# Recurrent layer's in-projections as float16 pairs, with block scales found on the chip

## The chip, the cores and the metric

The kernel runs on one core of one Trainium2 chip. The metric is the device time of one execution in microseconds; the kernel before took 1345.06 us (median of 3 runs, 1344.2 to 1348.67). Five engines work side by side, each through its own instructions in order: TensorE (PE, with its weight loads PEld), VectorE (DVE), ScalarE (ACT), GpSimd (POOL) and SyncE (SP), which issues the transfers.

## The reference, cut to what matters

Two layers process a prompt of 512 tokens and a sample of 32. Layer 0 mixes tokens by a recurrence (RWKV-7), layer 1 by differential attention. Each layer has one input projection, memory attention, a gate and an output projection.

```python
def rwkv_layer(x, mk, mv, prev_row, S0, norm_w, w_out, w_in, ...):
    h = rmsnorm(x, norm_w)
    p, qm, gate = jnp.split(h @ w_in, [RW_PROJ, RW_PROJ + MEM_W], axis=-1)
    y_mix, S_T, last_row = rwkv_mixer(p, prev_row, S0, ...)
    y_mem = mem_attention(qm, mk, mv)
    out = jnp.concatenate([y_mix, y_mem], axis=-1) * jax.nn.silu(gate)
    return x + out @ w_out, S_T, last_row
    ...
    def step(S, inp):
        r_t, k_t, v_t, w_t, kk_t, a_t = inp
        sa = jnp.einsum('bhvk,bhk->bhv', S, -kk_t)
        S = (S * w_t[:, :, None, :] + sa[..., None] * (kk_t * a_t)[:, :, None, :]
             + v_t[..., None] * k_t[:, :, None, :])
        return S, jnp.einsum('bhvk,bhk->bhv', S, r_t)
```

The change concerns `h @ w_in` of layer 0: 1024 rows by 7296 columns, for 544 tokens.

## The kernel before

All matrices stand with features on the 128 partitions and the 544 tokens along the free axis. The input projection of layer 0 is cut into 57 blocks of 128 output columns: 37 shifted rows (receptance, key, value for 12 head pairs, and one block for the low-rank parts), 4 queries, 16 gates. A block needs 1024 x 128 weights, 512 KB, in two half loads.

To keep float32 accuracy, an operand is split into a high and a low part, and a block is three products, high x high, high x low and low x high, over 8 slices of 128 rows and 2 halves of 272 tokens: 48 matmuls (`steps`, `gemm`). In layer 0 the parts are float32r, TensorE's faster float32 format: `hh`, `hl` for the normed tokens, `whi`, `wlo` for the weights. `split` makes the latter: ScalarE casts a half block, VectorE (the line `low.tensor_tensor`) subtracts. Layer 1 already uses float16 pairs. Since float16 has a narrow range, each weight block is scaled there by a power of two: `square_total` squares a half block on ScalarE with a running sum, `total_spread` adds the sums over the partitions by two one-column matmuls with a matrix of ones, `scales` takes the power of two on VectorE (three tiny instructions), `scaled` multiplies the raw block on GpSimd, `split_scaled` casts and subtracts, and the evacuation from PSUM multiplies by the inverse. `load_pair`, `measured`, `scaled_pool` belong to the same path; in the kernel before, `scaled_pool` is called between the layers.

Layer 0 runs in two parts. At the start (`inputs`, `lora_in`, three `shift` calls) the tokens are turned and normed, the memory keys are projected, and four in-projection blocks follow (36, 12, 0, 24). `weights` and `used` keep one split block and one loaded block ahead. There the order on each engine is left to the scheduler of the language. The remaining 53 in-projection blocks, the four memory value blocks and two output blocks form the generator `stream`: it loads two blocks ahead, and puts the casts and subtractions of the next block into a list of put-off work (`put_off`, `some`, `until`). From here on `self.ordered` holds, and each engine's order is that in which the program writes its calls.

What sets that order is the loop over 12 head pairs. Each pair runs a chain of 8 chunks in 23 links (`chunk`): TensorE multiplies, VectorE adds or ScalarE copies the result (`avz`, `sv`, `SB` are these operands), TensorE multiplies again. `PLAN` says which other work goes beside which link. Between links the loop issues matmuls of `stream`, spread by a reckoned time per matmul, `MAIN`, and per link, `HOP`; after each half link, `some` takes one or two put-off operations.

```python
while left and t + MAIN / 2 < (due[k + 1] if half else (due[k] + due[k + 1]) / 2):
    next(main)
    t += MAIN
    left -= 1
```

Of the kernel before, what the change touches and what calls it, by code (L numbers as in the profile page):

```python
# [43 lines left out]
STAT1, SPREAD1, POWER1, SCALE1 = (14, 27), 12, 32, (37, 41)  # L44
SPLITS2, SCALE2 = (7, 11, 13, 17), (33, 36)
# [32 lines left out]
HOP, MAIN = 0.27, 0.126  # L78
# [64 lines left out]
class Trunk:  # L143
# [190 lines left out]
    def square_total(self, rec, q):  # L334

        if q == 0:
            rec["st"] = self.sts[rec["n"] % 4]
            if rec["n"] < 3:
# [43 lines left out]
    def measured(self, rec):  # L382

        if "s" not in rec:
            for q in range(2):
                self.square_total(rec, q)
            ps = self.psx.tile([P, 512], F32, tag="x", name="ps_st")
            self.total_spread(rec, ps[:, 0:1], True)
            self.scales(rec)
            for q in range(2):  # L390
                self.scaled(rec, q)

    def split_scaled(self, rec):
# [4 lines left out]
        ks = [slice(q * KT // 2, (q + 1) * KT // 2) for q in range(2)]  # L398
        todo = [(lambda k=k: self.ae.copy(hi[:, k], raw[:, k]), 0.0) for k in ks]
# [77 lines left out]
    def proj(self, src, c0, evac):  # L477
        self.gemm([self.weights(src, c0)], [(self.hh, self.hl)], evac)
# [25 lines left out]
    def inputs(self):  # L504

        nc, a = self.nc, self.a
        with ExitStack() as ctx:
# [16 lines left out]
            self.ahead = [(a["w_mem_k"][0], 3 * P)] + [(a["rw_in"][0], j * P) for j in (36, 12, 0, 24)]  # L524
# [10 lines left out]
            self.consts_norm(parB)  # L535
            ss = p.tile([P, 7], F32, name="ss")
# [60 lines left out]
            for k in range(KT):  # L597
                h = p.tile([P, TP], F32, tag="hn", name="hn", bufs=3)
                self.ve.scalar_tensor_tensor(h[:], xT[k], self.nw[0][:, k : k + 1], pr[0][:], ALU.mult, ALU.mult)
                self.ae.copy(self.hh[:, k, :TP], h[:])  # L600
                (self.ve if k in (2, 5, 7) else nc.gpsimd).tensor_tensor(self.hl[:, k, :TP], h[:], self.hh[:, k, :TP].bitcast(F32), ALU.subtract)  # L601
                if k in (3, 6):
                    next(kv)
                if k == 1:
                    sh = [P, KT, TS]
                    hs = p.tile(sh, F32, name="hs")
                    self.ve.tensor_tensor(hs[:], xs[:], self.nw[0].unsqueeze(2).to_broadcast(sh), ALU.mult)
                    self.ve.tensor_tensor(hs[:], hs[:], pr[1][:, :TS].unsqueeze(1).to_broadcast(sh), ALU.mult)
                    self.ae.copy(self.hh[:, :, TP:], hs[:])
                    self.ve.tensor_tensor(self.hl[:, :, TP:], hs[:], self.hh[:, :, TP:].bitcast(F32), ALU.subtract)  # L610
# [8 lines left out]
    def shifted(self, j, tag, bufs, w=None):  # L619
# [4 lines left out]
        made = {}  # L624

        def evac(ps, v):
            self.ae.copy(raw[:, v.start + 1 : v.stop + 1], ps)
            if w is not None and v.start:
# [18 lines left out]
        if w is None:  # L647
            self.proj(self.a["rw_in"][0], j * P, evac)
# [426 lines left out]
    def gate(self, src, c0, g):  # L1075

        sg, _, evac = self.gate_evac(self.o1[g])
        self.proj(src, c0, evac)
        return sg

# [8 lines left out]
    def rw_finish(self, st):  # L1089
# [31 lines left out]
        self.ve.scalar_tensor_tensor(sg[:], sg[:], 0.5, bv[:], ALU.mult, ALU.mult)  # L1121
# [63 lines left out]
    def mem_block(self, i, kind, h, mh, ml, w, out, ps_pool, ps_tag):  # L1185
# [4 lines left out]
        ps = self.psg.tile([P, 512], F32, tag="g", name="ps_g")  # L1190
        for k in range(KT):
            for u, x in ((0, mh), (0, ml), (1, mh)):
# [7 lines left out]
                yield  # L1200

# [13 lines left out]

    def mem_head(self, i, h, w, cq, cg, p):

        st = {}
        it = self.mem_steps(st, i, h, p)
        for _ in range(3):  # L1220
            next(it)
        st["q"], evac = self.query_evac(p)
        self.proj(w, cq + h * P, evac)
        for _ in range(9):
            next(it)
        sg = self.gate(w, cg + h * P, 12 + h)
        st["gate"] = lambda: sg
        for _ in it:
            pass
# [267 lines left out]
    def layer0(self, mem):  # L1497
# [6 lines left out]
        with ExitStack() as ctx:  # L1504
# [40 lines left out]
            def add(pr, src, c0, make):  # L1545
                blocks.append((src, c0, make))
# [3 lines left out]
            def add_gate(pr, st, c0, n):  # L1550
                def make(wt):
                    sg, st["gate"], evac = self.gate_evac(self.sg[n % SGB])
                    yield from self.steps(wt, evac)
                add(pr, w, c0, make)

            def add_shift(pr, of, q):
# [3 lines left out]
                add(pr, w, (12 * q + of) * P, make)  # L1560

            def add_query(pr, h):
                def make(wt):
                    mems[h]["q"], evac = self.query_evac(self.ma if h % 2 else self.rb2)
                    yield from self.steps(wt, evac)
                add(pr, w, RW_PROJ + h * P, make)
# [40 lines left out]
            blocks += [b + (None,) for b in after[:2]]  # L1607

            def stream():
                raws = [self.load(*b[:2]) for b in blocks[:2]]  # L1610
                wt = self.split(raws.pop(0))
                for _ in wt[1]:
                    self.put_off(*_)
                for i, (_, _, make) in enumerate(blocks):
# [128 lines left out]
        with ExitStack() as ctx:  # L1743
# [45 lines left out]
            self.scaled_pool()  # L1789
# [24 lines left out]
    def scaled_pool(self):  # L1814

        nc, p = self.nc, self.h0
        self.hh, self.hl = (lambda t: (t[:, 0], t[:, 1]))(p.tile([P, 2, KT, T], F16, tag="hl", name="h16"))
# [15 lines left out]
        with nc.allow_low_precision("a bound, rounded before a power of two is taken from it"):  # L1833
            self.ae.activation(sq, self.nw[1], AF.Square, accum_out=st)
# [4 lines left out]
        self.ve.tensor_scalar(self.nwx, self.nw[1], sx, None, ALU.mult)  # L1839
# [664 lines left out]
    def run(self):  # L2504
# [15 lines left out]
        self.hh = hp.tile([P, KT, T], F32R, tag="hh", name="hh")  # L2520
        self.hl = hp.tile([P, KT, T], F32R, tag="hl", name="hl")
# [57 lines left out]
```

## Time and profile before

| | |
|---|---|
| median of 3 runs | 1345.06 us |
| profiled execution | 1347.07 us, its span 1345.4 us |
| mean granted TensorE clock | 0.991 of full speed |
| start and memory keys | 0 to about 45 us |
| recurrent layer | to about 700 us |
| output projection of layer 0 | about 700 to 800 us |
| layer 1 | about 800 to 1345 us |

Columns of the grouped rows are: line of the code (140 is a helper that all queues go through), engine, operation, output and inputs by tile name, shape and type, count; then busy us and mean ns of one; then the idle time of the engine just ahead of them and what ended it. In a timeline row come start, length (both us), engine, operation and how many alike follow each other. A matmul's length is a model that overlaps its neighbours, so distances between starts are the safer measure. The type `f32` on a matmul stands for both float32 and float32r; a plain float32 matmul leaves two records.

### The profile page before, as it was taken

To read this page: it belongs to the slowest core of one execution; us is meant where nothing else is said; L and a number is where in the kernel's file an instruction comes from. 1 tells how busy PE (TensorE), PEld (TensorE's weight loads), DVE (VectorE), ACT (ScalarE), POOL (GpSimd) and SP (SyncE) were. 2 spreads that over 40 slices of the span, in tenths; PEclk is the share of its full clock that TensorE was granted. 3 is DMA by queue.
4 is the path that set the end of the run, shared out by engine and by line. 5 is a ranking of instruction groups with operands and counts; after the bars stand their busy time and mean duration, and the time that the engine had idled before them with its cause. 6 is when DMAs were issued, how large, how long until landed. Compare 5 with 4: busy or idle time off the path is not lost. (4 is left out here: it accounts for less than half of the span.)

```text
span 1345.4 us, 32382 instructions
## 1 busy us (share of the span) xinstructions
PE 1298.5 (97%) x11786; PEld 1173.1 (87%) x11786; DVE 950.1 (71%) x2490; ACT 886.1 (66%) x2411; POOL 678.8 (50%) x1141
## 2 busy tenths in 40 slices
PE   6999999999999999999999999999999999999997
PEld 6998989999999999888899999888887887888885
DVE  6767667887787787767575355666698667987756
ACT  6665677777767867765554337777676776886652
POOL 1317765577557655860021007756555655654652
PEclk9999899999999999999999999999999999999999
DMA  7643223322322232233357445787777768774741
GB/s 235 188 114 82 62 71 88 79 70 78 88 64 69 77 99 64 63 96 98 108 158 215 131 130 152 166 186 156 165 175 169 171 159 183 171 169 111 223 150 67
DMA packets 417723, 171.56 MB, mean 128 GB/s; under 512 B 195145, under 2 KB 402514, under 8 KB 417562
## 3 DMA queue, kind: packets, MB, share of 16 engines
q1 hardware_dynamic: 417418, 168.96, 48.7%
q8 instruction: 93, 1.52, 0.5%
q14 instruction: 68, 0.56, 0.1%
q10 hardware_dynamic: 144, 0.52, 0.1%
HBM read 130.84 MB, written 41.92 MB: 128 GB/s over the span
## 5 line engine op out<-in xcount | busy, mean ns | idle before, releaser
L140 PEld LDWEIGHTS <-whs 128*128 128x128 f16 x3456 | 327.3, 98 | 67.4 <-issue 4.6
L140 PE MATMUL ps_g<-h,whs 128*128 128x272 f16 x2688 | 332.4, 279 | 1.0 <-POOL whs L140 1.0
L140 PE MATMUL ps_g<-hh,wlo 128*128 128x272 f32 x912 | 277.0, 304 | 1.5 <-DVE wlo L140 1.5
L140 PE MATMUL ps_g<-hh,whi 128*128 128x272 f32 x912 | 275.7, 303 | 0.9 <-ACT hh L140 0.9
L140 PE MATMUL ps_g<-hl,whi 128*128 128x272 f32 x912 | 271.7, 298 | 0.5 <-POOL hl L601 0.5
L890 POOL TENSOR_TENSOR tm<-u,m 102x84 f32<-102x84 f32 (+23 forms) x372 | 156.0, 419 | 166.2 <-DMA m<-sc 138.2
L140 PEld LDWEIGHTS ps_g<-hh,whi 128*128 128x128 f32 x912 | 174.8, 192 | 4.4 <-ACT hh L140 1.3
L140 PEld LDWEIGHTS ps_g<-hh,wlo 128*128 128x128 f32 x912 | 174.0, 191 | 4.9 <-DVE wlo L140 2.3
L140 PEld LDWEIGHTS ps_g<-hl,whi 128*128 128x128 f32 x912 | 174.1, 191 | 2.4 <-POOL hl L601 0.7
L892 POOL TENSOR_TENSOR u<-u,tm 102x84 f32<-102x84 f32 (+23 forms) x372 | 160.6, 432 | 29.1
L140 POOL TENSOR_TENSOR whs<-h16s,whs 128x512 f16<-128x512 f32 x126 | 147.6, 1189 | 48.3 <-ACT whs L140 46.6
L140 DVE TENSOR_TENSOR wlo<-raw,whi 128x512 fp32r<-128x512 f32 x178 | 128.4, 732 | 48.2 <-ACT whi L140 47.3
L140 ACT CAST whi<-raw 128x512 fp32r<-128x512 f32 x178 | 107.0, 616 | 35.4 <-issue 19.3
L140 POOL TENSOR_SCALAR h16s<-h16s 128x512 f32<-128x512 f32 x112 | 81.6, 741 | 93.7 <-DVE h16s L140 93.7
L140 ACT CAST whs<-h16s 128x512 f16<-128x512 f32 x144 | 84.8, 618 | 34.7 <-POOL h16s L140 33.1
L140 PE MATMUL ps_g<-hl,whs 128*128 128x272 f16 x768 | 94.1, 279 | 0.9 <-POOL whs L140 0.8
L140 ACT ACTIVATE junkw<-h16s 128x512 bf16<-128x512 f32 x138 | 86.5, 627 | 5.5 <-DMA h16s<-in_df_in_dram 4.9
L140 DVE SCALAR_TENSOR_TENSOR SB<-ps_c,dl,sd 64x64 f32<-64x64 f32 x168 | 47.4, 282 | 40.9 <-PE ps_c L140 37.4
L140 PE MATMUL ps_g<-lo,whi 128*128 128x272 f32 x256 | 73.9, 289 | 0.7 <-DVE lo L140 0.7
L140 PE MATMUL ps_g<-hi,whi 128*128 128x272 f32 x256 | 73.8, 288 | 0.7 <-ACT whi L140 0.7
L140 PE MATMUL ps_g<-hi,wlo 128*128 128x272 f32 x256 | 73.6, 288 | 0.2 <-DVE wlo L140 0.2
L140 ACT COPY sv<-ps_c 64x64 f32<-64x64 f32 x192 | 39.2, 204 | 39.8 <-PE ps_c L140 37.9
(420 smaller groups left out, 2943.6 us busy)
## 6 DMA issues: line engine op xcount, KB each, us to landing
raw<-in_rw_in_dram SPq DMA_DIRECT2D x114, 256.0 KB
h16s<-in_df_in_dram SPq DMA_DIRECT2D x112, 256.0 KB
raw<-in_w_out_dram SPq DMA_DIRECT2D x32, 256.0 KB
h16s<-in_w_out_dram SPq DMA_DIRECT2D x32, 256.0 KB
ptr<-pk SPq DMA_DIRECT2D x44, 160.0 KB
aT<-ptr SPq DMA_DIRECT2D x11, 640.0 KB
scr<-sg SPq DMA_DIRECT2D x96, 68.0 KB
out_dram<-scr SPq DMA_DIRECT2D x6, 1024.0 KB
```

What stands on the lines that cost most here:

```text
L140: return lambda *a, **k: self.trunk.tie(self, issue(*a, **k))
L890: nc.gpsimd.tensor_tensor(tm[:, :n, :wd], u3[:, :n, kx : kx + 1].to_broadcast(sh), m3[:, kx : kx + 1, kx + 1 :].to_broadcast(sh), ALU.mult)
L892: nc.gpsimd.tensor_tensor(u3[:, :n, kx + 1 :], u3[:, :n, kx + 1 :], tm[:, :n, :wd], ALU.add)
```

## The change

The 57 in-projection blocks of layer 0 go over to the float16 pairs of layer 1, with these differences (`self.plain`):

- `scaled_pool` is now called in `inputs` as well, for layer 0; the tokens `hh`, `hl` are float16 from the start.
- The raw block isn't multiplied by its scale on GpSimd. The scale goes into the cast (`activation` with a scale) and into the subtraction, which becomes a `scalar_tensor_tensor` on VectorE.
- Every block gets two squares on ScalarE, two one-column matmuls and three tiny VectorE instructions. In the stream the squares of block i + 3 are put off during block i, the one-column matmuls of block i + 2 go behind the 12th matmul of block i, its scale behind the 30th (`POWER0`).
- Loads of such blocks run up to four ahead instead of two, in four raw buffers in place of five half buffers. The squares' discarded output goes into another raw buffer for the first eight blocks, then into one fixed tile.
- Every evacuation multiplies by the inverse scale on ScalarE; the gate's factor one half takes it in.
- `MAIN` goes from 0.126 to 0.117.
- `gate` and `mem_head`, which nothing calls, are removed.

```diff
-HOP, MAIN = 0.27, 0.126
+HOP, MAIN = 0.27, 0.117
...
+            if self.plain:
+                if rec["n"] == 8:
+                    self.junk = self.wp.tile([P, KT, P], BF16, tag="wlo", name="junkw", bufs=2)[:]
+                rec["junk"] = self.raws[(rec["n"] + 1 + rec["n"] // 4) % 4].bitcast(BF16)[:, :, :P] if rec["n"] < 8 else self.junk
+            elif rec["n"] < 3:
...
+        if self.plain:
+            s, todo = rec["s"], []
+            for k in ks:
+                todo.append((lambda k=k: self.ae.activation(hi[:, k], raw[:, k], AF.Copy, scale=s), 0.0))
+                todo.append((lambda k=k: self.ve.scalar_tensor_tensor(lo[:, k], raw[:, k], s, hi[:, k], ALU.mult, ALU.subtract), LATER))
+            return (hi, lo, rec["inv"]), todo
...
         def evac(ps, v):
-            self.ae.copy(raw[:, v.start + 1 : v.stop + 1], ps)
+            self.ae.activation(raw[:, v.start + 1 : v.stop + 1], ps, AF.Copy, scale=w[2])
...
             def stream():
-                raws = [self.load(*b[:2]) for b in blocks[:2]]
-                wt = self.split(raws.pop(0))
...
+                bring(range(4))
+                squares = [lambda q=q: self.square_total(recs[2], q) for q in range(2)]
+                for fn in squares:
+                    self.put_off(fn)
+                wt, behind = self.split(recs[0]), None
...
                     self.until(todo[-1][0])
-                    if i + 2 < len(blocks):
-                        raws.append(self.load(*blocks[i + 2][:2]))
-                    nxt = self.split(raws.pop(0)) if raws else None
+                    for fn in squares[1:]:
+                        self.until(fn)
+                    if behind:
+                        self.scales(behind)
+                    bring(j for j in range(i + 2, i + 5) if j < i + 3 or j < len(blocks) and blocks[j][2] is not None)
+                    nxt = self.split(recs[i + 1]) if i + 1 < len(blocks) else None
...
+                    squares = [lambda q=q, rec=paired(i + 3): self.square_total(rec, q) for q in range(2)] if paired(i + 3) else []
+                    for fn in squares:
+                        self.put_off(fn)
+                    self.rec = behind = paired(i + 2)
...
-                        yield from make(wt)
+                        for n, _ in enumerate(make(wt)):
+                            yield
+                            if n == POWER0 and behind:
+                                self.scales(behind)
+                                behind = None
```

Three places show how instructions stand in a row before and now. The first is on ScalarE in the middle of layer 0, between two links of the chain of one head pair: `yt`, `sd` and `sv` are the chain's copies, `sg` the evacuation of a gate block, `whi` or `whs` the cast of a half block, `junkw` a square. Before:

```order
L140 COPY sv<-ps_c 64x64 x2
L140 COPY yt_104<-ps_c 64x128
L140 ACTIVATE sd<-SB_654,dl 128x128
L140 ACTIVATE sg_83<-ps_g 128x272
L140 CAST whi<-raw 128x512
L140 COPY sv<-ps_c 64x64 x2
```

Now, at the same link:

```order
L141 COPY sv<-ps_c 64x64 x2
L141 COPY yt_102<-ps_c 64x128
L141 ACTIVATE sd<-SB_682,dl 128x128
L141 ACTIVATE junkw,h16s<-h16s 128x512
L141 ACTIVATE sg_81<-ps_g,h16s 128x272
L141 ACTIVATE junkw,h16s<-h16s 128x512
L141 ACTIVATE whs<-h16s 128x512
L141 COPY sv<-ps_c 64x64 x2
```

Two squares have come between `sd` and the next `sv`.

The second is on VectorE in the same part: the subtractions `whs` of a block and the three instructions that make a later block's scale (`h16s`), ahead of the state update `SB`.

```order
L141 SCALAR_TENSOR_TENSOR whs<-h16s,whs 128x512
L141 TENSOR_TENSOR zr_87<-nk,de 128x4x128
L141 TENSOR_TENSOR zr_87<-nk,de 128x32
L141 TENSOR_SCALAR h16s<-ps_g 128x1
L141 TENSOR_SCALAR h16s<-h16s 128x1 x2
L141 SCALAR_TENSOR_TENSOR SB_679<-ps_c,dl,sd 64x64 x2
```

The three rows with `128x1` are new; they stand at once, not in the list of put-off work.

The third is on TensorE at the start, where the first in-projection block begins behind the memory key blocks (`mmh`, `mml`). Before:

```order
L140 MATMUL ps_g<-mmh,wlo 128x256
L140 MATMUL ps_mkt<-ident,memx 128x128 x2
L140 MATMUL ps_par<-ident,pA 128x121
L140 MATMUL ps_par<-ident,pC 128x38
L140 MATMUL ps_g<-hh,whi 128x272
L140 MATMUL ps_g<-hl,whi 128x272
```

Now:

```order
L141 MATMUL ps_g<-mmh,whi 128x256
L141 MATMUL ps_g<-mml,whi 128x256
L141 MATMUL ps_g<-mmh,wlo 128x256
L141 LDWEIGHTS h16s
L141 MATMUL ps_st<-h16s 128x1
L141 LDWEIGHTS whs
L141 MATMUL ps_g<-h_175,whs 128x272
```

A one-column matmul `ps_st` stands ahead of the first projection matmul. It is the fifth of eight at the start, the first half of the third in-projection block.

More of the change, by code (lines that the diff above doesn't have):

```diff
@@ L386, in measured @@
                 self.square_total(rec, q)
-            ps = self.psx.tile([P, 512], F32, tag="x", name="ps_st")
+            pool, tag = (self.psg, "g") if self.plain else (self.psx, "x")
+            ps = pool.tile([P, 512], F32, tag=tag, name="ps_st")
             self.total_spread(rec, ps[:, 0:1], True)
             self.scales(rec)
-            for q in range(2):
+            for q in () if self.plain else range(2):
                 self.scaled(rec, q)
@@ L523, in inputs @@
             self.early = [self.load(a["w_mem_k"][0], 2 * P)]
-            self.ahead = [(a["w_mem_k"][0], 3 * P)] + [(a["rw_in"][0], j * P) for j in (36, 12, 0, 24)]
+            self.ahead = [(a["w_mem_k"][0], 3 * P)] + [(a["rw_in"][0], j * P, 0) for j in (36, 12, 0, 24)]
             parA = self.params(
@@ L624, in shifted @@
         made = {}
+        ramp = w is None
+        if ramp:
+            w = self.weights(None, 0)
         def evac(ps, v):
-            self.ae.copy(raw[:, v.start + 1 : v.stop + 1], ps)
-            if w is not None and v.start:
+            self.ae.activation(raw[:, v.start + 1 : v.stop + 1], ps, AF.Copy, scale=w[2])
+            if not ramp and v.start:
                 self.put_off(tail)
@@ L1200, in mem_block @@
                 yield
+                n += 1
+                if n == SPREAD1 and self.rec is not None:
+                    self.total_spread(self.rec, ps[:, 480:481], False)
     def softmax(self, ps, n, p, tag, bufs):
@@ L1543, in layer0, with add @@
             blocks, each = [], [0] * NPAIR
-            def add(pr, src, c0, make):
-                blocks.append((src, c0, make))
+            def add(pr, src, c0, make, kind=None):
+                blocks.append((src, c0, kind, make))
                 if pr is not None:
@@ L1606, in layer0, with bring, paired @@
             after = self.w_out_blocks(0)
[L1607 removed]
+            blocks += [b + (None, None) for b in after[:2]]
             def stream():
[L1610 to L1611 removed]
+                recs = [None] * len(blocks)
+                def bring(js):
+                    for j in js:
+                        if j < len(blocks) and recs[j] is None:
+                            recs[j] = self.load(*blocks[j][:3])
+                def paired(j):
+                    return recs[j] if j < len(blocks) and blocks[j][2] is not None else None
+                bring(range(4))
[3 more added lines that the diff above has]
+                wt, behind = self.split(recs[0]), None
                 for _ in wt[1]:
                     self.put_off(*_)
[L1614 removed]
+                for i, (_, _, _, make) in enumerate(blocks):
                     wt, todo = wt
                     self.until(todo[-1][0])
[L1617 to L1619 removed]
+                    for fn in squares[1:]:
[4 more added lines that the diff above has]
+                    nxt = self.split(recs[i + 1]) if i + 1 < len(blocks) else None
                     for _ in nxt[1] if nxt else ():
                         self.put_off(*_)
+                    squares = [lambda q=q, rec=paired(i + 3): self.square_total(rec, q) for q in range(2)] if paired(i + 3) else []
+                    for fn in squares:
+                        self.put_off(fn)
+                    self.rec = behind = paired(i + 2)
                     if make is None:
```

61 lines of the change are left out of this document (23 added, 38 removed).

## The prediction

> **What bounds the kernel now.** I read the page first, for the engine that is never free.
>
> ```profile
> PE 1298.5 (97%) x11786; PEld 1173.1 (87%) x11786; DVE 950.1 (71%) x2490; ACT 886.1 (66%) x2411; POOL 678.8 (50%) x1141
> L140 PE MATMUL ps_g<-h,whs 128*128 128x272 f16 x2688 | 332.4, 279 | 1.0 <-POOL whs L140 1.0
> L140 PE MATMUL ps_g<-hh,wlo 128*128 128x272 f32 x912 | 277.0, 304 | 1.5 <-DVE wlo L140 1.5
> L140 PE MATMUL ps_g<-hh,whi 128*128 128x272 f32 x912 | 275.7, 303 | 0.9 <-ACT hh L140 0.9
> L140 PE MATMUL ps_g<-hl,whi 128*128 128x272 f32 x912 | 271.7, 298 | 0.5 <-POOL hl L601 0.5
> ```
>
> TensorE is busy for 97% of the span. The three rows with `hh` and `hl` are the products that the change turns to float16: 57 blocks of 48, that is 3 x 912 = 2736. The first `ps_g` row is layer 1, which already works on float16 pairs. The mean lengths overlap one another, so they say little; what a matmul costs is the distance between starts. Next, then, the busy time by stretches (us, busy PE, PEld, DVE, ACT, POOL with counts, clock, DMA share, GB/s).
>
> ```profile
> 33.00:50.00 17.00, 15.54 (x114) 14.20 (x113) 15.17 (x35) 9.57 (x24) 11.06 (x36) 1.00 0.65 191
> 200.00:550.00 350.00, 346.51 (x3524) 327.81 (x3524) 274.63 (x688) 256.50 (x737) 220.93 (x483) 0.99 0.30 78
> ```
>
> In the long middle of layer 0 TensorE lacks 3.5 of 350 us, VectorE works 78% and ScalarE 73%. So time saved per matmul shows in the total, as long as the other two keep up. The stretch from 33 to 50 us is the start, in which the first projection meets VectorE at 89%.
>
> **The pitch of a projection matmul.** From the timeline of TensorE, a run of 25 matmuls of layer 0 without anything between (first and last), and one of layer 1.
>
> ```profile
> 129.52 0.29 PE L140 MATMUL ps_g<-hl,whi 128*128 128x272 f32 x1
> ...
> 132.54 0.29 PE L140 MATMUL ps_g<-hl,whi 128*128 128x272 f32 x1
> 1264.24 0.19 PE L140 MATMUL ps_g<-h16s 128*128 128x1 bf16 x2
> 1264.30 2.94 PE L140 MATMUL ps_g<-hl,whs 128*128 128x272 f16 x24
> 1267.07 0.19 PE L140 MATMUL ps_g<-h16s 128*128 128x1 bf16 x2
> ```
>
> Layer 0: 3.02 us over 24 steps, 125.8 ns. Layer 1: 1264.30 to 1267.07 holds 24 matmuls, 115.4 ns. The difference is 10.4 ns. It need not hold where the matmul follows a small one, so I compare a group of scores and what comes after it in both layers.
>
> ```profile
> 606.93 1.03 PE L140 MATMUL ps_mm<-mhk,mq 128*128 128x256 f32 x4
> 607.61 0.48 PE L140 MATMUL ps_g<-hh,whi 128*128 128x272 f32 x1
> 607.92 0.29 PE L140 MATMUL ps_g<-hl,whi 128*128 128x272 f32 x1
> 887.89 1.03 PE L140 MATMUL ps_mm<-mhk,mq 128*128 128x256 f32 x4
> 888.75 2.94 PE L140 MATMUL ps_g<-h,whs 128*128 128x272 f16 x24
> 891.53 0.19 PE L140 MATMUL ps_g<-h16s 128*128 128x1 bf16 x2
> ```
>
> Group and first projection matmul take 0.99 us in layer 0; in layer 1 they take 3.64 less 23 x 0.1154, that is 0.99 us too. The first one after small work gains nothing. The timeline from 35 to 700 us has 317 such places, which leaves 2419 matmuls at 10.4 ns: **-25.2 us** (-28.5 if all 2736 gained).
>
> The Trainium skill ("TensorE: Matmul & The Clock Gate", Back-to-back issue gap) gives the distance of warm matmuls as the columns over 2.4 GHz plus 2.5 ns, with no word of the type: 115.8 ns here for both, so that this term would be zero. The trace agrees for float16 (115.4) and not for the float32 kind (125.8); the measurement decides.
>
> **What is added on TensorE.** Each of the 53 blocks of the stream brings two one-column matmuls that sum the squares. The pair at 1264.24 delays the next start by 0.06 us: 53 x 0.06 = **+3.2 us**.
>
> **What is added on ScalarE.** A half block's square, read out and followed by the next operation, in layer 1:
>
> ```profile
> 905.88 0.63 ACT L140 ACTIVATE junkw<-h16s 128x512 bf16<-128x512 f32 x1
> 906.41 0.19 ACT L140 ACTIVATION_READ_ACCUMULATOR junkw<-h16s 128x1 bf16 x1
> 906.50 0.96 ACT L140 ACTIVATE qp<-ps_g,h16s 64x272 fp32r<-64x272 f32 x2
> L140 ACT COPY raw<-ps_g 128x272 f32<-128x272 f32 x74 | 28.5, 386 | 30.9 <-PE ps_g L140 30.3
> L140 ACT ACTIVATE og<-ps_g,h16s 128x272 f32<-128x272 f32 x32 | 15.5, 485 | 8.7 <-PE ps_g L140 8.7
> ```
>
> 0.62 us of the engine each, 106 in the stream. An evacuation that scales takes 485 where a plain one takes 386 ns. The middle stretch holds 31 of the blocks (62 of the casts `whi`): 62 x (0.62 + 0.10) = 45 us, so ScalarE goes from 256 us in 350 to 301 in about 337: 89%. The casts stay as they are. It is still the smaller load; the question is what stands in front of the state chain's copies. There the trace shows room: end of the chain's copy `sv` against the start of the matmul that reads it, first and last of 72 such pairs between 200 and 550 us, and the tightest.
>
> ```profile
> 201.70 0.41 ACT L140 COPY sv<-ps_c 64x64 f32<-64x64 f32 x2
> 202.93 0.38 PE L140 MATMUL ps_c<-sv,bt 128*128 128x128 f32 x2
> ...
> 547.78 0.40 ACT L140 COPY sv<-ps_c 64x64 f32<-64x64 f32 x2
> 549.04 0.39 PE L140 MATMUL ps_c<-sv,bt 128*128 128x128 f32 x2
> ...
> 420.49 0.43 ACT L140 COPY sv<-ps_c 64x64 f32<-64x64 f32 x2
> 421.41 0.38 PE L140 MATMUL ps_c<-sv,bt 128*128 128x128 f32 x2
> L140 ACT COPY sv<-ps_c 64x64 f32<-64x64 f32 x192 | 39.2, 204 | 39.8 <-PE ps_c L140 37.9
> ```
>
> 0.82, 0.86 and 0.49 us of room behind the copy, and 39.8 us of idling over 96 copies of two, 0.41 each, ahead of it: about 1.25 us in all. One square fits. In the place of the order shown above, two squares stand between two links of the chain, 1.24 us more than before: just used up. So the cost is that of the crowded places: I take 0.4 us once in each of the 12 pairs, with VectorE's share below, **+4.5 us**. The ends: nothing, if the room holds everywhere; 72 us, if each of 96 links had two squares in front and only the tightest room (1.24 - 0.49). I take a value near the low end, since the typical row, not the tightest, decides, and 18 (a quarter of that) as the bad case in the range.
>
> **VectorE.** The split's low half becomes a three-operand instruction; the scale adds three tiny ones per block.
>
> ```profile
> L140 DVE TENSOR_SCALAR h16s<-h16s 128x1 int32<-128x1 int32 x129 | 23.2, 180 | 4.4
> L140 DVE TENSOR_SCALAR h16s<-ps_g 128x1 int32<-128x1 int32 x68 | 10.3, 152 | 11.5 <-ACT v L140 6.0 <-ACT k L140 3.7 <-ACT mq L140 1.4
> L140 DVE TENSOR_TENSOR rkv<-rkv,kf 128x544 f32<-128x544 f32 x12 | 8.8, 731 | 0.3
> L140 DVE SCALAR_TENSOR_TENSOR rkv<-raw,PA,rkv 128x544 f32<-128x544 f32 x36 | 28.1, 781 | 11.0 <-ACT raw L140 10.9
> L140 DVE SCALAR_TENSOR_TENSOR SB<-ps_c,dl,sd 64x64 f32<-64x64 f32 x168 | 47.4, 282 | 40.9 <-PE ps_c L140 37.4
> ```
>
> 0.152 + 2 x 0.180 = 0.51 us a block, and 781 - 731 = 50 ns for each low half: 31 x 0.51 + 62 x 0.05 = 19 us in the middle stretch, 294 in 337, 87%. Ahead of the state update `SB` VectorE idles 40.9 us over 84 pairs, 0.49 each, which covers the clump of three. Cost nothing while that holds; if the clump falls behind a long operation, the 0.5 us goes to the next link, and it is part of the 4.5. The clump reads a PSUM bank of `ps_g` 18 matmuls after the sum was written, about 2 us later, and so waits for nothing; behind it stand only the chain's operations.
>
> **Loads.** Four raw blocks instead of two and a half are in flight, the same bytes; at 30% of the DMA engines nothing is priced. Each load still precedes ScalarE's first touch by one block. The waits on SyncE's queue move with it.
>
> **The start.** Here the order puts a one-column matmul, which needs the squares of the third block, ahead of the first projection matmul. Each load of the start waits for the square of the block before it, whose discarded output lies in its buffer.
>
> ```profile
> 2.66 2.08 SPq L140 DMA_DIRECT2D raw<-in_w_mem_k_dram  x4
> 6.70 0.62 ACT L140 CAST whi<-raw 128x512 fp32r<-128x512 f32 x1 [1.22 <-DMA raw<-in_w_mem_k_dram]
> 31.05 0.59 ACT L140 COPY zr<-ps_t 128x512 f32<-128x512 f32 x1
> 35.37 0.39 PE L140 MATMUL ps_g<-hh,whi 128*128 128x272 f32 x1
> 44.62 0.68 ACT L140 COPY raw<-ps_g 128x272 f32<-128x272 f32 x2 [1.39 <-PE ps_g L140]
> ```
>
> A load lands about 3.5 us after its issue (one of the four ends its issue at 3.2, and the cast starts at 6.7). The first square stands behind the copy of 31.05: it ends at about 32.3. Load, square, load, square, 3.5 + 0.62 + 3.5 + 0.62, and about 2 us of ScalarE's casts between, put the first projection matmul at 42.5 instead of 35.4. It then runs without the waits that it has now, 48 x 0.115 = 5.5 us, to 48; before, it is done at 44.6. I take **+4.5 us** with its knock-on, between 0 (the loads land at once) and 9 (it starts when it now ends).
>
> **Sum.** -25.2 + 3.2 + 4.5 + 4.5 = -13.0 us. The profiled execution took 1347.07 (its span 1345.4 and 1.7 around it), 2.0 above the median of 1345.06 shown: 1334.1 for it, **1332 us** as a median.
>
> **Rivals.**
> - *The cover holds everywhere.* No crowded link, a start that loses 1 us: -25.2 + 3.2 + 1 = -21, 1324; with the whole 28.5 it would be 1321. For it: 1.25 us of room against 0.62. Against it: the doubled squares in the order. Chance 0.22.
> - *ScalarE comes late to the chain*, the slower side. Without the chain's share the sum is -17.5; over 96 links that is 0.18 us a link. Once squares delay the mean link by more than that, the change loses; at the 18 us of the bad case plus a start of 9 it is 1350. For it: 89% of ScalarE and 87% of VectorE beside a full TensorE, in order. Against it: the room measured above. Chance 0.21, half of it above 1349.
> - *The pitch doesn't fall* in layer 0: then only the additions are left, +12.2 us, 1357. The mechanism would be that something other than the matmul's type paces the runs there; the two runs quoted differ in type alone as far as the rows show. Chance 0.04. This is also where the rule of the Trainium skill's page "TensorE: Matmul & The Clock Gate" would lead.
> - The forecast itself, 1326 to 1340: 0.53.
>
> From these: faster by over 0.3% (below 1341; about what a measurement of this kernel can tell from no change) 0.75, within it 0.11, slower 0.14. The range from 1319 to 1350 leaves out the far ends of the first two rivals and the third.
>
> **What would show it.** Projection matmuls of layer 0 as f16 rows, 115 ns apart in runs: the first term. First projection matmul near 42 us: the start. ScalarE near 89% between 200 and 550 us, with TensorE's wait on `sv` and `yt` grown from almost nothing to a few us: the chain's term. If TensorE idles 15 us or more there, the room was misjudged. If the runs stay at 125 ns, the whole forecast is wrong.

## The result, and the profile after

The kernel before takes 1345.17 us (median of 4 runs, 1344.2 to 1348.67), the changed one 1390.32 us (1389.47 to 1394.08). The ratio is 1.0336, 95% interval 1.0309 to 1.0363: **45 us slower**, where 13 us faster was forecast, and outside the range. The profiled execution after the change has a span of 1392.4 us.

The page after, first the engines, then four groups of instructions that the forecast priced (busy us, mean ns of one, idle before and what ended it):

```profile
PE 1288.0 (93%) x11901; PEld 1092.5 (78%) x11901; DVE 987.4 (71%) x2673; ACT 977.6 (70%) x2641; POOL 669.3 (48%) x1142
L141 PE MATMUL ps_g<-h,whs 128*128 128x272 f16 x5424 | 709.7, 281 | 1.0 <-POOL whs L141 1.0
L141 ACT CAST whs<-h16s 128x512 f16<-128x512 f32 x144 | 84.8, 618 | 35.2 <-POOL h16s L141 33.6
L141 ACT ACTIVATE whs<-h16s 128x512 f16<-128x512 f32 x114 | 79.8, 716 | 0.3
L141 DVE SCALAR_TENSOR_TENSOR whs<-h16s,whs 128x512 f16<-128x512 f32 x114 | 89.5, 789 | 10.2 <-ACT whs L141 9.0
```

TensorE fell from 97% to 93% of a longer span. The projection matmuls are float16 rows now. The two `whs` rows of ScalarE are the plain cast (layer 1) and the cast with the scale inside (layer 0): 716 against 618 ns. The forecast had let the casts stay as they were.

The same two stretches as before, then the timeline of TensorE at a run of 14 projection matmuls of layer 0:

```profile
33.00:50.00 17.00, 14.59 (x93) 12.90 (x93) 13.74 (x35) 12.00 (x30) 10.69 (x32) 0.80 0.66 203
200.00:550.00 350.00, 320.49 (x3409) 267.06 (x3409) 280.49 (x731) 289.75 (x815) 204.77 (x471) 1.00 0.27 71
402.38 1.78 PE L141 MATMUL ps_g<-h,whs 128*128 128x272 f16 x14
```

The pitch came as forecast: 1.78 us less one matmul of 0.28, over 13 steps, is 115.4 ns. But TensorE now idles 29.5 of 350 us, where it lacked 3.5. ScalarE works 83% and VectorE 80% of the stretch: neither is full.

How long one pair of heads takes is read from an operation that occurs once a pair, ScalarE's `de`. Five pairs before, then five after:

```profile
319.61 0.67 ACT L140 ACTIVATE de<-cum 128x553 f32<-128x553 f32 x1
549.31 0.67 ACT L140 ACTIVATE de<-cum 128x553 f32<-128x553 f32 x1
300.03 0.66 ACT L141 ACTIVATE de<-cum 128x553 f32<-128x553 f32 x1
542.11 0.66 ACT L141 ACTIVATE de<-cum 128x553 f32<-128x553 f32 x1
```

229.7 / 5 = 45.9 us before, 242.1 / 5 = 48.4 after. The first of these `de` stands at 70.4 us before and at 85.4 after. So 15 us are lost in the start and 2.5 us in each of 12 pairs, 30 us. From the end of the recurrent layer on the two traces run alike: its last gate operation on VectorE starts 46.7 us later than before (752.0 against 705.3), and the span ends 47.0 later.

Who waits in the pairs now: some of the waits of VectorE, then of TensorE, from 200 to 550 us (us in total, times, longest). The last two rows are all that the same view lists for TensorE in the kernel before.

```profile
DVE h16s L141 <- ACT raw L141: 14.2, 7, 2.0
DVE SB L141 <- ACT bt L141: 7.2, 7, 1.0
DVE SB L141 <- ACT avz L141: 3.7, 7, 0.6
PE ps_c L141 <- DVE SB L141: 8.5, 7, 1.2
PE ps_w L141 <- DVE bv L141: 5.3, 7, 0.8
PE ps_y L141 <- DVE yt L141: 4.5, 6, 0.8
PE ps_c L141 <- ACT sv L141: 1.7, 8, 0.4
PE ps_y L140 <- DVE yt L140: 0.7, 3, 0.3
PE ps_w L140 <- DVE bv L140: 0.6, 3, 0.2
```

The first row is the scale's read of the sum, the operation of which the forecast said that it waits for nothing. It shares a PSUM tile with the projection's own result, and in this program it waits for ScalarE's evacuation of that tile, which was issued ahead of it. Of the 28 scales in this stretch seven wait, one in each pair. One of the seven, from the timelines of ScalarE and VectorE:

```profile
308.95 0.61 ACT L141 ACTIVATE junkw<-h16s 128x512 bf16<-128x512 f32 x1
309.68 0.49 ACT L141 ACTIVATE raw<-ps_g,h16s 128x272 f32<-128x272 f32 x1
310.21 0.16 DVE L141 TENSOR_SCALAR h16s<-ps_g 128x1 int32<-128x1 int32 x1 [2.02 <-ACT raw L141]
310.72 0.57 DVE L141 SCALAR_TENSOR_TENSOR SB<-ps_c,dl,sd 64x64 f32<-64x64 f32 x2
```

A square (`junkw`) stands on ScalarE ahead of the evacuation, the scale on VectorE stands behind the evacuation, and the state update `SB` stands behind the scale. TensorE's waits moved to what VectorE delivers (`SB`, `bv`, `yt`); the wait on ScalarE's `sv`, which the forecast watched, is 1.7 us.

### The profile page after: what moved, and what is told of

Read it like the earlier page. It is cut to its first block, busy times and chain, and to the rows that moved or that the text cites. A ratio compares the mean times of both kernels' runs of the same rounds, so it can differ in the third digit from the quotient of the medians.

```text
span 1392.4 us, 33058 instructions
## 1 busy us (share of the span) xinstructions
PE 1288.0 (93%) x11901; PEld 1092.5 (78%) x11901; DVE 987.4 (71%) x2673; ACT 977.6 (70%) x2641; POOL 669.3 (48%) x1142
## 4 chain that ended last, share of the span: by engine, by line
PE 50%; DVE 18%; ACT 16%; POOL 6%; issue 4%; DMA 4%; SPq 1%; DVEq 0%; ACTq 0%; POOLq 0%
PE ps_g L141 35%; PE ps_c L141 3%; ACT sv L141 2%; DVE whs L141 2%; POOL u L908 2%; ACT whs L141 2%; POOL tm L906 2%; PE ps_o L141 2%; ACT junkw L141 2%; PE ps_s L141 2%; POOL h16s L141 2%; DVE h16s L141 2%; SPq L141 1%; PE ps_at L141 1%; DVE SB L141 1%
## 5 line engine op out<-in xcount | busy, mean ns | idle before, releaser
L141 PE MATMUL ps_g<-h,whs 128*128 128x272 f16 x5424 | 709.7, 281 | 1.0 <-POOL whs L141 1.0
L141 PEld LDWEIGHTS <-whs 128*128 128x128 f16 x6192 | 587.1, 99 | 127.2 <-issue 10.9
L141 ACT ACTIVATE junkw<-h16s 128x512 bf16<-128x512 f32 x236 | 147.1, 624 | 5.8 <-DMA h16s<-in_df_in_dram 4.7
L141 DVE SCALAR_TENSOR_TENSOR whs<-h16s,whs 128x512 f16<-128x512 f32 x114 | 89.5, 789 | 10.2 <-ACT whs L141 9.0
L141 ACT ACTIVATE whs<-h16s 128x512 f16<-128x512 f32 x114 | 79.8, 716 | 0.3
L141 DVE TENSOR_TENSOR wlo<-raw,whi 128x512 fp32r<-128x512 f32 x64 | 45.7, 740 | 41.3 <-ACT whi L141 41.3
L141 ACT CAST whi<-raw 128x512 fp32r<-128x512 f32 x64 | 37.6, 618 | 32.4 <-issue 19.3
L141 POOL TENSOR_TENSOR h16s<-h16s,outf 128x512 f32<-128x512 f32 x32 | 37.1, 1179 | 46.6 <-DVE outf L141 43.0
L141 ACT ACTIVATE raw<-ps_g,h16s 128x272 f32<-128x272 f32 x74 | 36.0, 486 | 26.8 <-PE ps_g L141 25.8
L141 PE MATMUL ps_c<-sv,bt 128*128 128x128 f32 x192 | 40.0, 290 | 13.7 <-ACT yt L141 11.2
```

Of the source, the lines that this page charges most:

```text
L141: return lambda *a, **k: self.trunk.tie(self, issue(*a, **k))
```

## The experiments

Theory A: VectorE standing in order behind the evacuation makes the chain of states late. B: ScalarE's squares do. C: the longer casts and low halves do. R came up later: a second bound of the pair lies close beneath TensorE's, the ring of GpSimd's inverse for one (the inverse is stored, the next scores are made, stored and loaded, and the next inverse starts from them). Times are medians; the kernel before took 1344.5 to 1346.1 us beside them.

### One part of the scales at a time

**e1, the scale's read ahead of the evacuation.**

```diff
-POWER0 = 30
+POWER0 = 18
```

> The scale's three VectorE operations are issued 18 matmuls into a block instead of 30, that is ahead of ScalarE's evacuation of that half and not behind it; the rest is the changed kernel (1390 us). Theory A (VectorE stands still behind the evacuation, 14.2 us in the stretch from 200 to 550 us, and hands that on to the chain of states): VectorE's wait on the evacuation goes, 15 to 30 us less, 1360 to 1375 us. Theory B (ScalarE's squares come late to the chain): no change, 1387 to 1393. Theory C (the longer casts and low halves, 0.1 us of ScalarE and 0.05 us of VectorE each): no change. A rival to A is that the wait only changes sides: ScalarE's evacuation then waits for VectorE, and the time stays.

1461.7 us, ratio 1.0861 (1.0843 to 1.088). All theories missed; the rival named with them had the wait change sides to ScalarE, with the time unchanged. Waits of TensorE, 200 to 550 us:

```profile
PE ps_g L141 <- DVE h16s L141: 45.1, 25, 2.8
```

The wait changed sides, to the dearest place: the next projection matmul writes the tile that VectorE has yet to read, and TensorE stands still for VectorE, 1.8 us each time. In these two kernels, where the reader of the shared tile stands in the order decides who waits for whom.

**e2, no squares in the stream.**

```diff
-squares = [lambda q=q, rec=paired(i + 3): self.square_total(rec, q) for q in range(2)] if paired(i + 3) else []
+squares = []
+if paired(i + 3):
+    recs[i + 3]["st"] = self.sts[recs[i + 3]["n"] % 4]
```

> The squares of the 53 blocks of the stream are left out (each scale comes from the squares of one of the first four blocks, which stay); the one-column matmuls and VectorE's three operations stay. ScalarE has 106 x 0.62 = 66 us less. Theory B: the 53 us that the twelve pairs lost against the forecast come back almost whole, 1340 to 1350 us. Theory A: VectorE still waits for each evacuation, 1375 to 1390 us. Theory C: no change beyond 5 us.

1386.5 us, ratio 1.0296 (1.0275 to 1.0316): 4 us gained. B as the whole cause falls. How much the squares cost is less sure: the mean granted TensorE clock is 0.976 to 0.978 in these four runs, against 0.985 to 0.988 in those of the changed kernel, and that can hide a part of the gain (see the last section).

**e3, one scale for each kind of block.**

```diff
 def scales(self, rec):
+    if self.plain and rec["kind"] in self.fixed:
+        rec.pop("sum", None)
+        rec["s"], rec["inv"] = self.fixed[rec["kind"]]
+        return
...
-if n == SPREAD1 and self.rec is not None:
+if n == SPREAD1 and self.rec is not None and not (self.plain and self.rec["kind"] in self.fixed):
     self.total_spread(self.rec, ps[:, 480:481], False)
```

> The squares stay, but from the second block of each kind on the scale of the first is used: no one-column matmuls, no three operations on VectorE, no wait for the evacuation. Theory A: 1335 to 1355 us. Theory B: only the matmul pairs' 3 us and a little of VectorE, 1380 to 1388 us. Theory C: as B.

1378.2 us, ratio 1.0241 (1.0221 to 1.0261): 12 us gained. More than B and C gave, far less than A gave.

**e4, both e2's and e3's edits.**

> Both left out in the stream: no squares, no one-column matmuls, no scales but the first of each kind. What stays of the change are float16 matmuls, the scaled casts and low halves, and the start. Theories A and B: 1335 to 1345 us (the changed kernel less 53 us, and the start still costs 10 to 15). Theory C: over 1370 us. Two times above the sum of the two single gains or below it tell whether the two costs are one and the same.

1366.0 us, ratio 1.015 (1.0129 to 1.017). 24.4 us less than the changed kernel, where the two alone give 3.8 and 12.1. They seem not to be independent, though e2's lower clock may account for a part: the square of the quoted place delays the evacuation for which the scale waits. But 20 us above the kernel before are left, although TensorE's matmuls are as short as forecast; no theory expected that, so two questions opened: where the 25 us of the pitch are, and what else costs.

**e17, the scale's read long after the evacuation** (run late, since e1 had not taken the wait away).

```diff
-POWER0 = 30
+POWER0 = 44
```

> The changed kernel whole, but the scale's three VectorE operations are issued 44 matmuls into a block instead of 30, about 1.8 us later, when ScalarE has done the evacuation of the half that holds the sum. Nothing is left out. If VectorE's wait in order (14.2 us between 200 and 550 us) is the larger part of what the scales cost (e3 gained 12): 1372 to 1381 us. If the three operations themselves and the squares cost it, wherever they stand: 1386 to 1392.

1384.3 us, ratio 1.0294 (1.0278 to 1.0311): 6 us gained, between the two forecasts. VectorE's waits have no row for `h16s` any more:

```profile
DVE at L141 <- PE ps_at L141: 15.2, 15, 1.7
DVE SB L141 <- PE ps_c L141: 13.2, 17, 1.3
DVE SB L141 <- ACT bt L141: 5.8, 7, 0.8
```

So the wait in order was worth about 6 us of the changed kernel, not 53; the operations themselves, with the squares, are the larger part of the 24 us that e4 gained, by what is left over.

**e5, the raw block's load later in the block.** In the changed kernel SyncE waited 4.5 us a pair for a low half to free the buffer of the raw block four ahead, between the store of the finished inverse and that of the next scores (waits of its queue, 200 to 550 us):

```profile
SPq L141 <- DVE whs L141: 31.3, 7, 4.6
```

```diff
-bring(j for j in range(i + 2, i + 5) if j < i + 3 or j < len(blocks) and blocks[j][2] is not None)
+ahead = [j for j in range(i + 2, i + 5) if j < i + 3 or j < len(blocks) and blocks[j][2] is not None]
...
     yield
+    if n == 20:
+        bring(ahead)
```

> The changed kernel whole, but the load of the raw block four ahead is issued 20 matmuls into a block instead of at its start; on SyncE's queue it then stands behind the loads of the inverse (m<-sc) and no longer between the store of the finished inverse (sc<-u) and that of the next scores (sc<-at). Theory R (GpSimd's inverse is a closed ring that sets the pair: inverse, store, scores, loads, next inverse; in the changed kernel SyncE waits 4.6 us a pair in the middle of it, for VectorE's low half to free the raw buffer): the gap from the end of the inverse to the store of the scores falls from 7.7 to about 3 us, a pair from 48.2 to 44 to 45.5 us, in all 1350 to 1365 us. Theory A or B (VectorE's scale or ScalarE's squares late to the chain of states): no change, 1385 to 1392.

1406.4 us, ratio 1.0451 (1.043 to 1.0473): 16 us slower. Waits of SyncE's queue, 200 to 550 us:

```profile
SPq L141 <- DVE at L141: 36.5, 7, 6.1
```

With the load gone the same queue waits somewhat longer for the scores (`at`) themselves, which VectorE makes. The load had only been the last of two. Why it is 16 us slower, not equal, was not settled.

### Is TensorE the bound of a pair?

**e6, the kernel before with 4 of 48 matmuls left out.**

```diff
-self.te.matmul(ps[:, :TH], w[t][:, k, :], x[:, k, v], ...
+if x is self.hh or k not in (2, 5) or hasattr(self, "nwx"):
+    self.te.matmul(ps[:, :TH], w[t][:, k, :], x[:, k, v], ...
```

> The kernel before, with 4 of the 48 matmuls of each of layer 0's 53 stream blocks left out (products of the low half of the activations with the high half of the weights, for two of eight row blocks); nothing else changes. That is 212 x 0.1258 = 26.7 us of TensorE, a little more than what the float16 pitch was to save. If TensorE alone bounds the pairs (the ground of the forecast): 1317 to 1322 us. Theory R (the ring of the inverse bounds the pair at the same 45.4 us): 1338 to 1346 us, no change.

1342.5 us, ratio 0.997 (0.9959 to 0.998). 26.7 us of TensorE's work are gone and 3.7 come out. The places of the left-out matmuls stay in the order of calls. The middle stretch and TensorE's largest wait in it:

```profile
200.00:550.00 350.00, 334.68 (x3452) 313.84 (x3451) 278.50 (x692) 259.18 (x745) 221.45 (x495) 1.00 0.30 78
PE ps_c L140 <- DVE avz L140: 7.4, 15, 1.0
```

This run shows that what the forecast rested on was wrong in the kernel *before* the change: the freed time turns into waits at once, with nothing added anywhere. It shows this for the order of calls as it is; another order was not tried.

**e10, the float16 pairs and nothing else:** weights unscaled, plain casts and low halves, loads two ahead, no squares or scales at all.

```diff
-todo.append((lambda k=k: self.ae.activation(hi[:, k], raw[:, k], AF.Copy, scale=s), 0.0))
-todo.append((lambda k=k: self.ve.scalar_tensor_tensor(lo[:, k], raw[:, k], s, hi[:, k], ALU.mult, ALU.subtract), LATER))
+todo.append((lambda k=k: self.ae.copy(hi[:, k], raw[:, k]), 0.0))
+todo.append((lambda k=k: self.ve.tensor_tensor(lo[:, k], raw[:, k], hi[:, k], ALU.subtract), LATER))
...
-bring(range(4))
+bring(range(2))
```

> What is left of the change when all that finds and applies scales of the weights is taken out: float16 pairs of the unscaled weights with plain casts and plain low halves, loads two blocks ahead as before. TensorE has its 25 us less. If TensorE were what holds the pairs: 1318 to 1324 us. As e6_before_fewer took 27 us of TensorE away and gained 3.7, I expect the same here: 1338 to 1345 us. If the longer casts are not part of the loss, it stays where e9 is, above 1350.

1342.6 us, ratio 1.0 (0.9969 to 1.0031): no difference that can be told. It agrees with e6, by another way: the pitch is real and is worth next to nothing here.

**e7, e8, e11, e12, the inverse stopped early:** e4, the kernel before, e10 and e6, each with

```diff
-for kx in range(31):
+for kx in range(23):
```

> As e4_neither (no squares, no scales in the stream; 1366 us), and GpSimd's inverse stops after 23 of its 31 columns, so that it is about 5 us shorter in each pair. Theory R: the ring is shorter, TensorE bounds again with its float16 pitch, a pair takes 43.5 to 44 instead of 45.7 us: 1340 to 1350 us. Every theory that puts the loss into ScalarE, VectorE or the longer casts: 1362 to 1367.

> The kernel before with the same shorter inverse (23 of 31 columns). If ring and TensorE both stand at 45.4 to 45.7 us a pair, as theory R has it, shortening the ring alone brings nothing: 1338 to 1346 us. If the ring alone had been the bound in the kernel before, 12 pairs times up to 5 us would go: 1290 to 1310.

> e10_pairs_only with GpSimd's inverse stopped after 23 of 31 columns (5 to 7 us a pair). If the ring of the inverse is the second bound beside TensorE (in e6_before_fewer its four pieces add up to 45.0 us, the length of a pair): 1315 to 1326 us. If the fixed order of the chain's operations on VectorE and ScalarE is the second bound: within 4 us of e10.

> The kernel before with both: 4 of 48 matmuls of layer 0's blocks left out (e6_before_fewer, 1342 us) and the inverse stopped after 23 of 31 columns (e8_before_cut, 1344 us). If TensorE and the ring are two bounds at the same height, taking down either brings 2 to 4 us and both together 20 to 27: 1318 to 1326 us. If something else is the second bound: 1337 to 1343.

1365.3 (ratio 1.0146, 1.0127 to 1.0164), 1344.3 (0.9989, 0.9978 to 1.0), 1340.4 (0.9961, 0.9946 to 0.9976) and 1339.1 us (0.9954, 0.9939 to 0.9969): each within 4 us of the kernel without the cut. In e8 SyncE's queue has no wait for the inverse left, so the ring did get its slack, and the time hardly moved. The ring of the inverse, which I had taken for *the* second bound, is not it alone; by e11's expectation that points to the order of VectorE's and ScalarE's operations.

**e15 and e16, VectorE's low halves left out**, on e10 and on e11.

```diff
+if self.ordered:
+    lo = self.hl[:, :, :P]
```

> e10_pairs_only (1343 us), with VectorE's low halves of the stream's blocks left out: a slice of the activations' low half stands in for the weights' low half, and VectorE has 106 x 0.72 = 76 us less. If VectorE's operations, in their fixed order, are the second bound beside TensorE: 1316 to 1326 us. If it is the ring of the inverse or the latency of the chain of states: 1337 to 1343.

> e15_pairs_nolow with the inverse stopped after 23 of 31 columns. If VectorE and the ring are two further bounds at nearly one height: 10 to 20 us below e15, 1312 to 1325. If e15 is at TensorE's bound already: within 4 us of e15. If it is the chain's own latency: still 1336 to 1343.

1334.1 us (ratio 0.9922, 0.9899 to 0.9945) and 1327.6 us (0.9871, 0.9857 to 0.9886). e15 lies between its two forecasts: VectorE's share gives 8 us. The 6.5 that e16 takes off on top, where the shorter inverse gave 2 without, are not shown to be the ring's as a limit: they go with TensorE's granted clock. The ten runs of e15 lie between 1328.1 and 1344.9 us, at mean granted clocks from 0.987 down to 0.976; its two runs at 0.987 took 1328.1 and 1328.9, hardly longer than the four of e16 (1325.8 to 1328.5, at 0.988 and 0.989). The six runs of e10 at 0.988 and 0.989 took 1341.1 to 1344.5, so at like clocks VectorE's low halves are worth about 14 us and the shorter inverse 1 or 2. The middle stretch of e10, e15 and e16 (busy PE, PEld, DVE, ACT, POOL, then the granted clock):

```profile
200.00:550.00 350.00, 333.56 (x3552) 282.05 (x3550) 279.14 (x693) 262.13 (x739) 220.52 (x494) 0.99 0.30 79
200.00:550.00 350.00, 337.91 (x3527) 288.19 (x3526) 235.29 (x623) 261.31 (x736) 206.75 (x500) 0.95 0.30 78
200.00:550.00 350.00, 334.38 (x3582) 286.80 (x3580) 245.14 (x638) 264.94 (x749) 162.63 (x384) 0.98 0.30 77
```

This fits two limits at nearly one height, TensorE and VectorE's order, each of which hides what is saved on the other. That the ring is a third is not shown; the shorter inverse may only have spared the clock. With all three lowered, 17 us come out. What holds the other 8 of TensorE's 25 was not settled; the clock column is a candidate for a part (last section).

### The start, and the casts

**e9, e4 with one constant scale in the start too** (no squares, one-column matmuls or chained loads there).

```diff
 def scales(self, rec):
+    if self.plain:
...
+        rec["s"], rec["inv"] = self.fours, self.fixed[kind]
+        return
...
+nc.gpsimd.memset(self.fours, 1024.0)
```

> As e4_neither (1366 us), and in the start too: one fixed scale (1024) for every block, so that the four first blocks have no squares, no one-column matmuls and no loads chained behind squares. Loads stay four ahead, scaled casts stay. If the start is worth what it looks like in the traces (the first projection matmul 10 us later, and all of it kept to the end): 1353 to 1358 us. If the pairs take it back (the later stream is bound elsewhere): 1363 to 1367.

1346.5 us, ratio 1.0018 (1.0 to 1.0036): 19.5 us less than e4, twice what was expected.

**e13, the changed kernel with a constant scale in its first four blocks**, and **e14, its squares' discarded output in PSUM**, so that no load waits for a square.

```diff
 def measured(self, rec):
+    if self.plain:
+        rec["s"], rec["inv"] = self.fours, self.fouri
+        return
```

```diff
+if self.plain:
+    rec["psj"] = ps[:].rearrange("p (k c) -> p k c", c=P)
...
-self.ae.activation(rec["junk"][:, k], rec["raw"][:, k], AF.Square, ...
+self.ae.activation(rec["psj"] if "psj" in rec else rec["junk"][:, k], rec["raw"][:, k], AF.Square, ...
```

> The changed kernel whole, but the four first blocks take a constant scale (1024): no squares, no one-column matmuls, no loads chained behind squares in the start; the stream finds its scales as changed. By e9 against e4 the start is worth 19.5 us: 1368 to 1373 us. If it is only the 10 us by which the first projection matmul comes later: 1379 to 1382.

> The changed kernel, but the discarded squares of the four first blocks go to the PSUM tile of their sum and not to the buffer of the block after, so that no load waits for a square; squares and one-column matmuls stay. If the chained loads make the start late (load, square, load, square, 3.5 + 0.6 us each): most of e13's gain, 1370 to 1378 us. If the squares behind ScalarE's casts, and TensorE's one-column matmuls that wait for them ahead of the projection, make it late: under 3 us gained, 1386 to 1391.

1385.2 us (ratio 1.0303, 1.0286 to 1.032) and 1385.0 us (1.0299, 1.0278 to 1.032). Both 5 us better, so the chained loads were the larger part of what the start can give back while the stream is as changed; e13 missed its 20. Its first `de` comes 8.2 us earlier than in the changed kernel (77.2 against 85.4), in e9 13.2 us earlier than in e4 (68.1 against 81.3). It still comes 9.1 us later in e13 than in e9, although neither finds scales in the start: the stream's own squares and scales already delay it.

**e18, e17 and e14 together,** the best version that computes everything.

> e17 and e14 together: scale issued late, the start's loads not chained behind squares; the whole computation. If the two add (e14 gained 5): 5 us below e17, 1367 to 1377 if the wait in order was it, else 1381 to 1387. Against the kernel before (1345) it stays slower by every theory, since TensorE's 25 us do not show (e6, e10).

1377.1 us, ratio 1.0237 (1.0218 to 1.0257): the two gains add, 13 us, and it stays slower than the kernel before. No run that finds its scales on the chip beats the kernel before.

## Why the prediction was wrong

The 45 us come apart in four steps, each the difference of two runs:

| what is added | from, to | us |
|---|---|---|
| float16 pairs alone | before (beside e10) 1345.3, e10 1342.6 | -2.8 |
| scale inside casts and low halves, loads four ahead | e10, e9 1346.5 | +3.9 |
| scales of the start | e9, e4 1366.0 | +19.5 |
| squares, sums and scales of the stream | e4, changed 1390.3 | +24.4 |

The first two are uncertain by some 4 us each (the intervals of e10 and e9); their sum, e9 against before, is 1 to 2. The split between the last two depends on the order of taking things away: in the changed kernel the scales of the start give back 5 us (e13), and then 39 are left for the stream. Against the forecast of -13 the 58 us of error are 22.4 for the pitch, 16.7 for the stream (24.4 against 4.5 and 3.2), 15 for the start and 3.9 for casts, low halves and loads.

- **"So time saved per matmul shows in the total"**, the step from 97% busy to bound, is where it failed first. The pitch fell by the forecast 10.4 ns, and -25.2 became -2.8, give or take 4. An engine that is 99% busy in a stretch is *a* bound; e6 shows that it was not the only one. The best supported other one is VectorE's fixed order (e10 against e15); the whole of it stays open. A view of the kernel before had looked like a sign of the ring, SyncE's waits between 200 and 550 us: 60 us for the end of GpSimd's inverse, 7.5 us in each pair, before the next scores could go. e8 took that wait away and gained under 2 us, so a wait in a queue is not yet a bound.

```profile
SPq L140 <- POOL u L892: 60.4, 8, 9.3
```

- **"The clump ... so waits for nothing"** was wrong. The row quoted there for `h16s<-ps_g` had the answer: layer 1's scale idles 11.5 us, mostly for ScalarE's `v`, `k` and `mq`, the evacuations of the same PSUM tile. I read the mean of 152 ns and not the idle time behind it. e17 prices that wait at 6 us.
- **The chain's cover, +4.5 us** with a bad case of 18, is, with the +3.2 for the one-column matmuls, the term that was mis-sized most beside the pitch: 24.4 together. Room was measured at ScalarE's link alone (`sv`), and squares and scale were priced apart; e2, e3 and e4 (4, 12, 24) point to more than a sum of the two, as far as the lower clock of e2 allows to say. Slips in the working change little: 12 times 0.4 is 4.8, not 4.5, and the stretch holds 61 of the `sv` pairs, not 72; the rows quoted for them stand. The rival on the slower side had the right sign and the wrong engine: TensorE waits for VectorE's `SB`, `bv` and `yt`.
- **The start, +4.5**, was 19.5 beside a free stream and 5 in the changed kernel. The sum of loads and squares was near (first projection matmul forecast at 42.5, seen at 45.37), but I had the delay made good by a smooth block behind it. TensorE stood again, for the fourth block's square:

```profile
45.37 0.51 PE L141 MATMUL ps_g<-h,whs 128*128 128x272 f16 x3
57.90 0.16 PE L141 MATMUL ps_st<-h16s 128*128 128x1 bf16 x1 [6.10 <-ACT h16s L141]
```

- **"The casts stay as they are"** put at nothing what took 98 ns more on each of 114; with the low halves and the loads it is the 3.9 us of the table, uncertain as said.
- **+3.2 us for the one-column matmuls** was not tested by itself. In the changed kernel's trace, 200 to 550 us, a pair of them delays the next start by at most 0.06 us in 23 of 30 places, as forecast, and by 0.20 to 0.23 in seven.
- The pitch did fall, 115.4 ns against 125.8. The rule of the Trainium skill ("TensorE: Matmul & The Clock Gate", Back-to-back issue gap), by which it would not, is not what happened.

## What to carry to other kernels

Before an engine's saved time is put into a sum, ask of the kernel as it is whether less work on that engine shortens it: leaving out a twelfth of the projection's matmuls would have told here that some 25 us are worth 3 or 4. Where a tuned order has brought several engines to one height, as it seems here, added work on the others costs at once, while saved work on one is not paid out. And an operation that reads a corner of a shared tile can wait for another user of the tile that stands ahead of it, as the scale did here for 2 us once a pair: read its idle time in the page, not only its duration.

## What was not expected of the hardware

Where TensorE idles or runs tiny matmuls for a moment, its granted clock (the share of full speed that it is given) can fall, and the matmuls that follow take nearly twice as long. In the start of the changed kernel, TensorE's clock by stretches, and a group of the memory matmuls between 30 and 46 us before and after (min, median, max ns):

```profile
33.00:36.00 3.00, 2.73 (x16) 2.63 (x16) 2.44 (x5) 3.00 (x9) 1.31 (x2) 0.65 0.82 234
42.00:45.00 3.00, 3.00 (x19) 2.91 (x19) 2.58 (x10) 1.80 (x5) 2.49 (x10) 0.64 1.03 328
L140 PE MATMUL ps_g<-mmh,whi x12: 278/283/363, 29.7 to 34.4; 128*128 128x256 f32 x12
L141 PE MATMUL ps_g<-mmh,whi x16: 278/415/562, 33.3 to 45.0; 128*128 128x256 f32 x16
```

After two waits close together, of 0.94 us and, for a square, 1.44 us, the distance of these matmuls goes from 0.12 (second and third row of the timeline below) to 0.21 us (fourth and fifth), and back to 0.11 or 0.12 (the last two) some 3.4 us later; in between, from 34 to 37 us, the granted clock is 0.50. So the start pays twice for a short wait: first the wait, then the clock.

```profile
33.27 0.16 PE L141 MATMUL ps_st<-h16s 128*128 128x1 bf16 x1 [1.44 <-ACT h16s L141]
...
33.62 0.28 PE L141 MATMUL ps_g<-mmh,wlo 128*128 128x256 f32 x1
33.74 0.28 PE L141 MATMUL ps_g<-mmh,whi 128*128 128x256 f32 x1
...
34.65 0.41 PE L141 MATMUL ps_g<-mmh,wlo 128*128 128x256 f32 x1
34.86 0.41 PE L141 MATMUL ps_g<-mmh,whi 128*128 128x256 f32 x1
...
37.41 0.28 PE L141 MATMUL ps_g<-mmh,wlo 128*128 128x256 f32 x1
37.52 0.28 PE L141 MATMUL ps_g<-mmh,whi 128*128 128x256 f32 x1
```

The Trainium skill ("TensorE: Matmul & The Clock Gate", Part 1: The HAM clock gate) has the array at half its clock until it has been busy for some 3.4 us, which gives, as an estimate from that page, 256 columns over 1.2 GHz, 213 ns; the trace agrees with its 0.21 us and the 3.4 us.

The same happens inside the pairs, and it may take back a part of what is saved on TensorE. In e10 TensorE waits for VectorE, runs 32x32 matmuls, and then projects at (1.54 - 0.28) / 5 = 0.25 us:

```profile
307.22 0.24 PE L141 MATMUL ps_w<-t1b,at 32*32 32x32 f32 x2 [0.72 <-DVE t1b L141]
307.68 0.93 PE L141 MATMUL ps_w<-t1b,at 32*32 32x32 f32 x30 [0.22 <-DVE t1b L141]
308.55 1.54 PE L141 MATMUL ps_g<-h,whs 128*128 128x272 f16 x6
```

In e15 the mean clock of the middle stretch is 0.95 (quoted above), that is about 350 x 0.05 = 17 us of full clock lost, where e16 at 0.98 loses 7. The kernel before has 0.99. The idle time of the stretch does not decide it: TensorE idles 12.1 us in e15 at 0.95, but 15.3 in e6 and 29.5 in the changed kernel at 1.00; so when a wait costs the clock, and when not, is left open.

Time and clock also go together from run to run of one kernel. The ten runs of e10 reach from 1337.6 us at a mean clock of 0.992 to 1357.3 at 0.975, and those of e9 and e15 spread in the same way, while all runs of the kernel before lie between 0.990 and 0.996. The one run of e10 with a clock like that took some 8 us less than the kernel before beside it. Whether the lower clock makes a run long, or the waits of a long run lower its clock, is not shown; either way a few microseconds between two medians say little before their clocks are compared.
